# Six PSUM banks as three score tiles and three transposed groups where attention scores are narrow

## The chip, the cores and the metric

The kernel runs on one core of one Trainium2 chip. A core has five engines that run their own instruction streams and wait for each other through semaphores: TensorE (PE in the profile; PEld is its weight load), VectorE (DVE), ScalarE (ACT), GpSimd (POOL) and SyncE (SP), which issues the DMAs here. Matrix products land in PSUM, eight banks of 512 float32 columns for each of 128 partitions; everything else lies in SBUF or in device memory. The metric is the device time of one execution in microseconds (us), as the median of several runs.

## The reference, cut to what matters

One layer: a gated feed-forward block, a token mixer with two attentions side by side, and a second feed-forward block, for 1024 tokens and 1024 channels in float32. The two attentions are what the change touches.

```python
# differential attention: 8 heads, two score maps each, causal
s = einsum('bqhcd,bkhcd->bhcqk', qb, k) * scale          # c = 0, 1
p = softmax(where(kpos <= qpos, s, NEG_INF))
a = p[:, :, 0] - lam * p[:, :, 1]
o = einsum('bhqk,bkhe->bqhe', a, v)
...
# sparse attention: 16 heads in 2 groups, three branches with gates
o_cmp = ...   # over compressed blocks of keys
o_slc = ...   # causal, over selected key blocks (with 16 blocks in all, every causal one)
o_win = ...   # causal, over a window of 512 keys
o = g[..., 0:1] * o_cmp + g[..., 1:2] * o_slc + g[..., 2:3] * o_win
```

For query block i of 128 rows a causal score map has w = 128 * (i + 1) columns, from 128 to 1024; the window's has at most 640.

## The kernel before, in words

Float32 products are made of two parts of each operand, a rounded one ("hi") and the rest ("lo"), so most matrix products appear three times (L52, L53, L54). The phases follow each other: the first feed-forward block, preliminaries of the mixer (projections, the compressed branch), the differential attention `da_phase`, the sparse attention `ns_phase`, the output projections, the second feed-forward block.

Both attention phases have the same shape. The work of a head is cut into four steps m of two query blocks (z = 0, 1). `scores` makes one score map of one query block: matmuls into a PSUM tile S (L871), on VectorE the mask and the row minimum (L878, in place in S), on ScalarE the exponential (L880), which reads S and writes the probabilities to SBUF (Pt in the differential phase; Ps and Pw, selected and window branch, in the sparse one). That read is the last use of S. `tr_split` then transposes up to four 128x128 blocks of probabilities into one PSUM bank (tr, L926) and splits them into th (ScalarE, L89) and tl (VectorE, L85); matmuls with the values add them up in another bank, o (L948 to L950 in the differential phase, L1083 and L1084 in the sparse one; L1049 starts the sparse o with the compressed branch). The scores of step m are written into the program ahead of `finish` of step m - 1, the part with the transposes, so scores run ahead of the products.

Between the steps a `Filler` puts projections that later phases need: 24 matmuls into one bank (gm), a few of them after each query block. They have a lower priority than the attention's instructions, and each is held behind the last score matmul emitted so far (`K.gate = K.last`). In the differential phase they are many, in the sparse phase few: six matmuls a query block.

A Tile framework makes semaphores and order: it takes the program's instructions by priority (mostly their order in the program) as soon as their operands and a buffer of their pool are ready in its own model of time, and the order that it so finds for each engine is fixed in the compiled program. A pool has a number of buffers; a tile waits until one is free. Pools are opened with `reuse_waits="tile"`: where a new pool takes the space of a closed one, its tiles wait for the tiles that lay there.

PSUM during both attentions, before: two score tiles of two banks each (`sp1`, `sp2`), two transposed groups (`tr1`, `tr2`), one o, one gm, on the left side one after the other. A score map of more than 512 columns fills half of each of two banks; a narrower one lies in the first bank only. During the preliminaries four banks on the right side belong to `gm0`, and the other four on the left; the last projections of the preliminaries are emitted at the head of `da_phase`, still in `gm0`, before `cg.close()` closes that pool. Each of them is emptied by VectorE through single SBUF buffers that are stored to device memory.

SBUF buffers around it: 7 score rows (Pt) in the differential phase and 5 of each kind in the sparse one; 2 and 3 buffers each of th and tl.

Of the kernel before, what the change touches and what calls it, by code (L numbers as in the profile page):

```python
# [7 lines left out]
F32 = mybir.dt.float32  # L8
# [10 lines left out]
P = 128  # L19
T = 1024  # L20
TB = 512
# [22 lines left out]
def open_pool(K, ctx, name, bufs, psum=False, side=None):  # L44
    kw = {"space": PSUM} if psum else {}
    if side:
        kw["side"] = side
    return ctx.enter_context(K.tc.tile_pool(name=name, bufs=bufs, reuse_waits="tile", **kw))
# [813 lines left out]
        nc.sync.dma_start(out=K.s_pc[u * 2 + pr][tb], in_=pp.bitcast(F32))  # L862


def scores(K, passes, w, mask, nm, pt, l):
    nc = K.nc
    S = K.sp.tile([P, T], F32, tag="S", name="S")
    pieces = [(0, 0, w)] if w <= TB else [(0, 0, w // 2), (TB, w // 2, w // 2)]
    for o, c, n in pieces:
        for i, (q, k, k0) in enumerate(passes):  # L870
            K.last = nc.tensor.matmul(S[:, o:o + n], lhsT=q, rhs=k[:, k0 + c:k0 + c + n], start=i == 0, stop=i == 1)  # L871
    if w <= TB:
        sv, mv, pv = S[:, 0:w], mask, pt[:, 0:w]
    else:
        sv = S.rearrange("p (b c) -> p b c", b=2)[:, :, 0:w // 2]
        mv = mask.rearrange("p (b c) -> p b c", b=2)
        pv = pt[:, 0:w].rearrange("p (b c) -> p b c", b=2)
    nc.vector.tensor_tensor_reduce(out=sv, in0=sv, in1=mv, scale=-0.125, scalar=BIG, op0=ALU.add, op1=ALU.min,  # L878
                                   accum_out=nm)
    return nc.scalar.activation(out=pv, in_=sv, func=AF.Exp, scale=-1.0, bias=nm, accum_out=l)  # L880
# [81 lines left out]
def da_finish2(K, h, H, ob, sq):  # L962
    nc = K.nc
    tot = K.tr.tile([P, TB], F32, tag="tr", name="tot")
    nc.tensor.matmul(tot, lhsT=K.ones, rhs=sq, start=True, stop=True)
    m = K.op.tile([P, TB], F32, tag="sq", name="m")
    nc.vector.tensor_scalar(out=m, in0=tot, scalar1=1.0 / P, scalar2=EPS, op0=ALU.mult, op1=ALU.add)
    y = K.op.tile([P, TB], F32, tag="yr", name="yr")
    z = K.op.tile([P, TB], F32, tag="zr", name="zr")
    newton_rsqrt(nc, y, z, m, nc.gpsimd)  # L970
    nc.vector.scalar_tensor_tensor(out=ob, in0=ob, scalar=K.hgain[:, h:h + 1], in1=y, op0=ALU.mult, op1=ALU.mult)
    yo = [K.op.tile([P, TB], F32R, tag=t, name="yo") for t in ("yr", "zr")]
    split(nc, yo[0], yo[1], ob)
    for i in range(2):
        nc.sync.dma_start(out=K.s_yda[H][h][:, i], in_=yo[i].bitcast(F32))


def da_load(K, h):
    drain([da_load_parts(K, h)])
# [320 lines left out]
TR_DA = 2  # L1300
# [4 lines left out]
def da_phase(K, cg):  # L1305
    nc = K.nc
    with ExitStack() as ctx:
        K.kp, K.vp, K.qp = open_pool(K, ctx, "dk", B_DK), open_pool(K, ctx, "dv", B_DV), open_pool(K, ctx, "dq", B_DQ)
        K.nk, K.vv = {}, {}
        for n, f in enumerate(da_units(K, 0)[:2] + da_units(K, 1)):  # L1310
            if n == 2:
                early = da_load_parts(K, 0)
            if n >= 2:
                next(early)
            if n == 5:
                q0 = da_queries(K, 0, 0)
            drain([f()])
        cg.close()
        K.low = LOW_DA
        log_exp(K)  # L1320
        K.pp, K.sm, K.tp, K.op = (open_pool(K, ctx, "dp", B_DP), open_pool(K, ctx, "dsm", 6), open_pool(K, ctx, "dt", B_DT),
                                  open_pool(K, ctx, "do", 1))
        K.sp = open_pool(K, ctx, "sp1", 2, True)
        K.tr = open_pool(K, ctx, "tr1", TR_DA, True)
        K.ops = open_pool(K, ctx, "o1", 1, True)
        K.gm = open_pool(K, ctx, "gm1", 3 - TR_DA, True)
        pend = K.fin = None

        def finish(h, m, res):
            if m % 2 == 0:  # L1330
                K.o = K.ops.tile([P, TB], F32, tag="o", name="o")
            if K.fin:
                da_finish2(K, *K.fin)
                K.fin = None
            da_pv(K, h, m, res, K.o)
            if m % 2 == 1:
                K.fin = da_finish(K, h, m // 2, K.o)

        ng = NG_DA // 2
        W = K.A["win"]  # L1340
        units = []
        for p in (2, 3):
            cs = [[C_QDA + 2 * p, C_QDA + 2 * p + 1], [C_KDA + 2 * p, C_KDA + 2 * p + 1], [C_VDA + 2 * p], [C_VDA + 2 * p + 1]]
            units += [(f, [W[c] for c in ws]) for f, ws in zip(da_units(K, p), cs)]
        units += [(f, [W[C_GATE + c]]) for c, f in enumerate(gate_units(K, range(16)))]
        units += [(lambda d=d: pda_unit(K, d), [K.A["wda"][d]]) for d in range(KD)]
        fill = K.filler = Filler(K, units)
        for p in range(4):
            fill.pace(4 * (p + 1) if p < 2 else 8 + ng * (p - 1), PACE_DA)
            for h in (2 * p, 2 * p + 1):  # L1350
                if h:
                    da_load(K, h)
                for m in range(4):
                    qt = q0 if h + m == 0 else da_queries(K, h, m)
                    if h == 4:
                        ns_load_key(K, m)
                    res = da_scores(K, h, m, qt, fill.step)
                    if pend:
                        finish(*pend)
                    pend = (h, m, res)  # L1360
            fill.end()
        finish(*pend)
        da_finish2(K, *K.fin)


def ns_phase(K):
    nc = K.nc
    K.low = LOW_NS
    with ExitStack() as ctx:
        K.wslab = open_pool(K, ctx, "wsl", 1).tile([P, 5 * P], F32, name="wslab")  # L1370
        nc.sync.dma_start(out=K.wslab, in_=K.A["wslab"])
        K.qp, K.kp, K.pcp = open_pool(K, ctx, "nq", 2), open_pool(K, ctx, "nk", 1), open_pool(K, ctx, "npc", B_NPC)
        K.pp, K.sm, K.tp, K.op = (open_pool(K, ctx, "np", B_NP), open_pool(K, ctx, "nsm", 6), open_pool(K, ctx, "nt", B_NT),
                                  open_pool(K, ctx, "no", B_NO))
        K.sp = open_pool(K, ctx, "sp2", 2, True)
        K.tr = open_pool(K, ctx, "tr2", 2, True)
        K.ops = open_pool(K, ctx, "o2", 1, True)
        K.gm = open_pool(K, ctx, "gm2", 1, True)
        fill = K.filler
        fill.pace(8 + 16 + KD, PACE_NS)  # L1380
        ns_load_values(K)
        pend = None

        def finish(hd, m, res, st, g, par):
            if m % 2 == 0:
                K.o = K.ops.tile([P, TB], F32, tag="o", name="o")
            ns_pv(K, hd, m, res, K.o, st[0], g, par)
            if m % 2 == 1:
                ns_fold(K, par, K.o, st[1])
                if par:  # L1390
                    ns_out(K, hd // 2, m // 2, st[1])

        for g in range(2):
            for pr in range(4 * g, 4 * g + 4):
                for H in range(2):
                    pc = K.pcp.tile([P, 2, TB], F32R, tag="pc", name="pc")
                    nc.sync.dma_start(out=pc.bitcast(F32), in_=K.s_pc[pr][H])
                    y = K.op.tile([P, TB], F32, tag="y", name="y")
                    for par in range(2):
                        hd = pr * 2 + par  # L1400
                        qt = []
                        for z in range(2):
                            t = K.qp.tile([P, TB], F32R, tag=f"q{z}", name="qt")
                            nc.sync.dma_start(out=t.bitcast(F32), in_=K.s_qns[hd // 4][z:z + 2, :, hd % 4, :, H * TB:(H + 1) * TB]
                                              .rearrange("h a d t -> (h a) d t"))
                            qt.append(t)
                        for m in (2 * H, 2 * H + 1):
                            res = ns_scores(K, hd, m, qt, g, fill.step)
                            if pend:
                                finish(*pend)  # L1410
                            pend = (hd, m, res, (pc, y), g, par)
        fill.end()
        if pend:
            finish(*pend)


def proj(K, open_x, after):
# [54 lines left out]
def body(tc, A, out):  # L1472
    nc = tc.nc
    K = Ctx()
    K.tc, K.nc, K.A = tc, nc, A
    K.low, K.vv, K.gate, K.fill, K.seen = 0, {}, None, None, {}
    K.h, K.acc, K.R = [None] * 2, [None] * 2, [None] * 2
    with ExitStack() as ctx:
        const = open_pool(K, ctx, "const", 1)
# [172 lines left out]
```

## Time and profile before

| | |
|---|---|
| median of 3 runs | 2951.38 us (2950.32 to 2952.54) |
| the profiled execution | 2957.75 us, span 2955.7 us |
| TensorE busy | 2830.8 us, 96% of the span |
| VectorE, ScalarE, GpSimd busy | 68%, 46%, 27% |
| mean granted TensorE clock | 0.986 |
| first and last score matmul (L871) of the differential phase | 972.0 us, 1449.1 us |
| last score matmul of the sparse phase | 2070.4 us |

A row of the timeline holds the start in us, the duration in us, engine, line and operation, the tiles (out<-in), the shape, how many instructions are merged ("x4"), and in brackets the idle time of the engine before it and what ended it. A row of the table of stretches holds start and end, then the busy us of each engine with the number of instructions, the granted clock, the share of the DMA engines and GB/s. A row of the waits holds engine, line and what it waited for, the us in total, how many times, and the longest.

### The profile page before, as it was taken

Reading aid. Unit: us, or ns where it says so; the run is one execution under the profiler, and the core shown is the slowest. Engines: PE = TensorE matmul, PEld = TensorE weight load, DVE = VectorE, ACT = ScalarE, POOL = GpSimd, SP = SyncE. Lnnn points to the kernel's source line nnn. Section 1 sums busy time; section 2 is a strip of 40 time slices with the busy share of each in tenths; the row PEclk is TensorE's granted clock in tenths of the full one; section 3 lists DMA queues with packets and bytes.
Section 4 is the critical chain, followed back from the end, with each engine's and each line's share of the span. In section 5 each row is a group of like instructions: output and inputs, shape, how many; then the busy total and the mean of one; then the engine's idle time right before and its main releaser. Section 6 shows DMA issues by size and latency. Waiting matters only on the chain. (4 is left out here: it accounts for less than half of the span.)

```text
span 2955.7 us, 40158 instructions
## 1 busy us (share of the span) xinstructions
PE 2830.8 (96%) x14276; PEld 2129.2 (72%) x14276; DVE 2002.1 (68%) x3347; ACT 1366.1 (46%) x2347; POOL 788.7 (27%) x701
## 2 busy tenths in 40 slices
PE   8999999999999899989899999999999999999998
PEld 6644447888888678778788888888778854444886
DVE  7866856666687467667677777776343877675666
ACT  7543424442332245445466666666332653342443
POOL 3133321000144123322233323332242413333001
PEclk9999999999999999999999999999999999999999
DMA  4355548655456544444332234222742246454854
GB/s 161 129 194 180 182 161 287 214 172 170 146 200 240 173 161 168 170 165 164 122 115 79 86 119 155 79 84 76 281 158 100 89 147 230 149 185 158 297 182 146
DMA packets 212711, 478.20 MB, mean 162 GB/s; under 512 B 20896, under 2 KB 39584, under 8 KB 212512
## 3 DMA queue, kind: packets, MB, share of 16 engines
q1 hardware_dynamic: 212512, 475.65, 47.1%
q8 instruction: 112, 1.84, 0.3%
q14 instruction: 87, 0.71, 0.1%
HBM read 313.56 MB, written 162.00 MB: 161 GB/s over the span
## 5 line engine op out<-in xcount | busy, mean ns | idle before, releaser
L405 PEld LDWEIGHTS <-w 128*128 128x128 f16 x3024 | 297.1, 99 | 381.1 <-issue 30.4
L52 PE MATMUL gm<-hi,whi 128*128 128x512 f32 x880 | 351.5, 399 | 4.0 <-ACT whi L89 1.6
L54 PE MATMUL gm<-hi,wlo 128*128 128x512 f32 x880 | 348.3, 397 | 1.1 <-DVE wlo L85 1.1
L53 PE MATMUL gm<-lo,whi 128*128 128x512 f32 x880 | 348.0, 395 | 0.0
L405 PE MATMUL Y<-tf,w 128*128 128x512 f16 x1296 | 296.7, 383 | 19.1 <-DVE u L443 15.6
L871 PE MATMUL S<-kt,qt 128*128 128x320 f32 (+5 forms) x1152 | 274.6, 352 | 37.5 <-ACT Pt L880 12.0
L85 DVE TENSOR_TENSOR tl<-tr,th 128x512 fp32r<-128x512 f32 (+2 forms) x384 | 236.3, 619 | 89.0 <-ACT th L89 85.5
L89 ACT ACTIVATE th<-tr 128x512 fp32r<-128x512 f32 (+2 forms) x384 | 203.7, 542 | 200.4 <-PE tr L926 195.6
L85 DVE TENSOR_TENSOR wlo<-st,whi 128x1024 fp32r<-128x1024 f32 x154 | 197.6, 1300 | 113.5 <-ACT whi L89 112.2
L878 DVE CUSTOM_DVE_ANT_0 S<-S,slab 128x896 f32<-128x896 f32 (+7 forms) x320 | 224.7, 709 | 65.8 <-PE S L871 61.3
L53 PE MATMUL acc<-wlo,whi 128*128 128x512 f32 (+1 forms) x628 | 244.1, 389 | 1.0 <-DVE wlo L85 1.0
L89 ACT ACTIVATE whi<-st 128x1024 fp32r<-128x1024 f32 x154 | 160.7, 1057 | 178.2 <-PE acc L54 111.6
L54 PE MATMUL acc<-whi,wlo 128*128 128x512 f32 (+1 forms) x628 | 242.8, 389 | 0.0
L52 PE MATMUL acc<-whi 128*128 128x512 f32 (+1 forms) x628 | 240.4, 387 | 0.0
L871 PEld LDWEIGHTS S<-kt,qt 128*128 128x128 f32 x1152 | 183.4, 190 | 61.5 <-ACT Pt L880 13.8
L1037 POOL TENSOR_SCALAR Ps<-Ps,l 128x384 f32<-128x384 f32 (+7 forms) x128 | 100.7, 787 | 428.6 <-DVE l L1035 214.4
L405 PE MATMUL X<-h,w 128*128 128x512 f16 x864 | 195.3, 379 | 0.5 <-ACT s L415 0.5
L52 PEld LDWEIGHTS gm<-hi,whi 128*128 128x128 f32 x880 | 168.3, 191 | 37.2 <-ACT whi L89 2.2
L54 PEld LDWEIGHTS gm<-hi,wlo 128*128 128x128 f32 x880 | 167.8, 191 | 37.3 <-DVE wlo L85 1.8
L53 PEld LDWEIGHTS gm<-lo,whi 128*128 128x128 f32 x880 | 168.1, 191 | 30.9
L85 DVE TENSOR_TENSOR wlo<-wst,whi 128x1024 fp32r<-128x1024 f32 x103 | 135.8, 1320 | 45.4 <-ACT whi L89 36.1
L1083 PE MATMUL o<-th,vt 128*128 128x256 f32 (+1 forms) x608 | 165.0, 288 | 1.6 <-ACT th L89 1.5
(320 smaller groups left out, 6128.7 us busy)
## 6 DMA issues: line engine op xcount, KB each, us to landing
wst<-in_win_dram SPq DMA_DIRECT2D x55, 512.0 KB
sw<-w2s SPq DMA_DIRECT2D x44, 512.0 KB
st<-sw SPq DMA_DIRECT2D x88, 256.0 KB
st<-saT SPq DMA_DIRECT2D x88, 256.0 KB
a<-in_f1w_dram SPq DMA_DIRECT2D x36, 512.0 KB
a<-in_f2w_dram SPq DMA_DIRECT2D x36, 512.0 KB
st<-saB SPq DMA_DIRECT2D x66, 256.0 KB
qt<-sq SPq DMA_DIRECT2D x128, 128.0 KB
```

The costliest lines, as they stand in the source:

```text
L52: first = nc.tensor.matmul(out, lhsT=w[0][:, wk], rhs=x[0], start=start, stop=False, skip_group_check=skip)
L53: nc.tensor.matmul(out, lhsT=w[0][:, wk], rhs=x[1], start=False, stop=False, skip_group_check=skip)
L54: nc.tensor.matmul(out, lhsT=w[1][:, wk], rhs=x[0], start=False, stop=stop, skip_group_check=skip)
L85: return nc.vector.tensor_tensor(out=lo, in0=src, in1=hi.bitcast(F32), op=ALU.subtract)
L89: nc.scalar.activation(out=hi, in_=src, func=AF.Copy)
L405: K.mark = nc.tensor.matmul(o, lhsT=w[:, a, m * h + k], rhs=x[k][:, b], start=start and k == 0 and i == 0, stop=k == h - 1 and i == 2, ski ...
L871: K.last = nc.tensor.matmul(S[:, o:o + n], lhsT=q, rhs=k[:, k0 + c:k0 + c + n], start=i == 0, stop=i == 1)
L878: nc.vector.tensor_tensor_reduce(out=sv, in0=sv, in1=mv, scale=-0.125, scalar=BIG, op0=ALU.add, op1=ALU.min, accum_out=nm)
L1037: nc.gpsimd.tensor_scalar(out=p[:, 0:n], in0=p[:, 0:n], scalar1=l[:, c:c + 1], scalar2=1.0, op0=ALU.mult, op1=ALU.mult)
L1083: nc.tensor.matmul(dst, lhsT=v, rhs=hi[:, b * P:(b + n) * P], start=False, stop=False, skip_group_check=True)
```

## The change

`scores` takes its tile from a new function `score_tile`. It keeps two layouts of six banks: for w up to 512 three score tiles of one bank and three transposed groups, for wider ones two score tiles of two banks and two groups as before. Where the layout of the wanted tile isn't the open one, both pools are closed and opened anew, on the right side of PSUM. o and gm stay open, on the left side, which puts them in banks 0 and 1. In the differential phase steps m = 0, 1 of a head are narrow and m = 2, 3 wide; in the sparse phase the first half of the queries (two heads, m = 0, 1) is narrow and the second half wide, as the window's 640 columns are wide too. So the layout changes twice in each of 8 heads of the one and twice in each of 8 pairs of heads of the other. The transposes of a step are emitted after the next step's scores, so they take their group from the layout of that next step.

```diff
+def score_tile(K, w):
+    n = 1 if w <= TB else 2
+    if K.s_banks != n:
+        close_scores(K)
+        K.sp, K.s_banks = open_pool(K, K.s_ctx, "sp", (3, 2)[n - 1], True, side="right"), n
+        K.tr = open_pool(K, K.s_ctx, "tr", (3, 2)[n - 1], True, side="right")
+    return K.sp.tile([P, n * TB], F32, tag="S", name="S")
+
+
+def close_scores(K):
+    K.s_ctx.close()
+    K.s_ctx, K.s_banks = ExitStack(), 0
+
+
 def scores(K, passes, w, mask, nm, pt, l):
     nc = K.nc
-    S = K.sp.tile([P, T], F32, tag="S", name="S")
+    S = score_tile(K, w)
...
 # da_phase
-        K.sp = open_pool(K, ctx, "sp1", 2, True)
-        K.tr = open_pool(K, ctx, "tr1", TR_DA, True)
...
         da_finish2(K, *K.fin)
+        close_scores(K)
...
 # ns_phase
-        K.sp = open_pool(K, ctx, "sp2", 2, True)
-        K.tr = open_pool(K, ctx, "tr2", 2, True)
...
             finish(*pend)
+        close_scores(K)
...
 # body
+    K.s_ctx, K.s_banks = ExitStack(), 0
```

## The prediction

> **What bounds the kernel now.** I read the page first, then the table of stretches cut at each change of score width, then the waits of TensorE, then the timeline at three places.
>
> ```profile
> span 2955.7 us, 40158 instructions
> PE 2830.8 (96%) x14276; PEld 2129.2 (72%) x14276; DVE 2002.1 (68%) x3347; ACT 1366.1 (46%) x2347; POOL 788.7 (27%) x701
> ```
>
> TensorE (PE) is the bound: no other engine passes 68%. The change alters no matmul, so all it can move is PE's idle time while the two attentions run, from about 968 to 2109 us. The vector engine's score operation (L878) shows the widths, and I cut there. The four sums are: differential attention narrow (up to 512 columns) and wide, sparse attention narrow and wide, eight stretches each; under them one neighbouring pair of the sparse phase.
>
> ```profile
> core 0: us, PE busy (x) PEld busy (x) DVE busy (x) ACT busy (x) POOL busy (x), PEclk, DMA share, GB/s
> sum 254.20, PE 230.55 PEld 196.51 DVE 159.83 ACT 104.47 POOL 63.36; mean PE 28.82 PEld 24.56 DVE 19.98 ACT 13.06 POOL 7.92
> sum 249.90, PE 232.77 PEld 194.11 DVE 178.50 ACT 128.66 POOL 66.70; mean PE 29.10 PEld 24.26 DVE 22.31 ACT 16.08 POOL 8.34
> sum 295.50, PE 276.40 PEld 240.99 DVE 200.12 ACT 169.94 POOL 77.25; mean PE 34.55 PEld 30.12 DVE 25.01 ACT 21.24 POOL 9.66
> sum 336.30, PE 330.56 PEld 298.59 DVE 250.32 ACT 221.68 POOL 110.61; mean PE 41.32 PEld 37.32 DVE 31.29 ACT 27.71 POOL 13.83
> 1539.50:1578.20 38.70, 35.99 (x233) 31.48 (x233) 26.87 (x77) 21.61 (x57) 9.90 (x16) 1.00 0.21 78
> 1578.20:1616.10 37.90, 37.47 (x246) 34.13 (x244) 30.69 (x70) 26.08 (x54) 13.80 (x16) 1.00 0.27 90
> ```
>
> Sum less PE busy is PE's idle time: 23.7 and 17.1 us in the differential phase, 19.1 and 5.7 us in the sparse one. The pair shows the pattern there: a narrow stretch idles 2.7 us, a wide one 0.4 us. So 42.8 us of idle lie where buffers are added. Next, what ended PE's waits, first from 1477.7 to 2037.9 us (sparse), then from 974 to 1477 us (differential).
>
> ```profile
> PE S L871 <- ACT Ps L880: 7.1, 14, 1.0
> PE o L1049 <- DVE y L1093: 5.2, 7, 1.1
> PE o L1084 <- DVE tl L85: 4.0, 15, 0.3
> PE S L871 <- ACT Pw L880: 3.3, 8, 0.9
> PE o L1083 <- ACT th L89: 0.7, 4, 0.2
> ```
>
> ```profile
> PE S L871 <- ACT Pt L880: 12.0, 8, 5.7
> PE o L948 <- ACT th L89: 6.8, 2, 3.9
> PE tr L653 <- DVE vt L650: 3.7, 2, 2.6
> ```
>
> A score matmul that waits for an exponential (Ps, Pw, Pt, L880) waits for a score tile to come free: 10.4 us in the sparse phase. In the differential phase it is 12.0 us, but one wait of 5.7 us is half of that, and it stands behind ScalarE, which waits there for the store of a filler's tile:
>
> ```profile
> 1269.37 0.60 ACT L89 ACTIVATE vh<-tr 128x512 fp32r<-128x512 f32 x1 [5.61 <-DMA sv<-vh]
> ```
>
> **The change part by part.** It adds and removes no engine instruction and no DMA; it changes which tile waits for which.
>
> *Three score tiles where they are narrow.* The clearest case is the step from wide to narrow:
>
> ```profile
> 1538.96 0.44 PE L871 MATMUL S<-kt,qt 128*128 128x128 f32 x2 [0.22 <-ACT Ps L880]
> 1540.51 0.44 PE L871 MATMUL S<-kt,qt 128*128 128x128 f32 x2 [0.78 <-ACT Ps L880]
> 1539.99 0.37 ACT L880 ACTIVATE Ps<-S,nm 128x128 f32<-128x128 f32 x1 [0.22 <-DVE nm L878]
> 1543.87 0.79 ACT L880 ACTIVATE Pw<-S,nm 128x640 f32<-128x640 f32 x1
> ```
>
> The last wide tile is held until ScalarE reads it at 1543.87, so the second narrow tile waits for the first one's exponential (1539.99), 0.78 us. In the new layout one freed wide tile makes room for two narrow ones, and this wait goes. The 10.4 us are the most that goes; nothing is the least, if the next wait ends as late: the third tile again waits for 1543.87. I take 6.5 us, nearer to the upper end, because the 0.78 us recur in each sparse narrow stretch and the wide stretches, where PE has other work, idle so little. The Trainium skill ("Perfetto Trace Analysis", Optimization Strategy) says that the same gap repeating on the engine that should be saturated can mean that there isn't enough SBUF or PSUM for the next tile. By it the whole idle of the eight sparse stretches, 19.1 us, would fall to the wide ones' 0.4 us each, a gain of 15.9 us in place of my 8 us (this edit and the next), and the sum below would be -16 us.
>
> *Three transposed groups.* The waits for th and tl in the sparse phase are 4.0 + 0.7 us. A third PSUM group helps only until the split's output, which keeps its three buffers there (two in the differential phase); the 5.2 us of L1049 wait for the output bank, which stays single. Bounds: 4.7 us gained, or 2 us lost (half of the tl waits again) when PE's order puts transposes ahead of products. I take a gain of 1.5 us.
>
> *Other narrow waits of the differential phase.* Here the fillers' 24-matmul products keep PE fed. Bounds: the 5.7 us wait goes and so does a second of its kind (3.9 us), or one more such wait arises (4 us lost). I take a gain of 2 us, the 12.0 us less 5.7 us, a third of it.
>
> *The new wait at a switch.* Six banks as 3 + 3 and as 4 + 2 overlap in one bank: a transposed group of the narrow layout sits where half of a wide score pair will be. Whether a new pool waits for the old pool as a whole or tile by tile shows at the old boundary between the phases: the sparse phase's mask, the first tile in the space of the closed pools, is loaded while their last scores still run.
>
> ```profile
> L1371 SPq DMA_DIRECT2D wslab<-in_wslab_dram x1: 424/424/424, 1442.6 to 1442.6; - x1
> 1449.09 1.17 PE L871 MATMUL S<-kt,qt 128*128 128x512 f32 x4
> ```
>
> So I take it tile by tile. Then one wide pair is free at once and the other waits for the last narrow group. What that means in the sparse phase:
>
> ```profile
> 1577.40 0.74 PE L871 MATMUL S<-kt,qt 128*128 128x320 f32 x4
> 1579.48 0.86 PE L871 MATMUL S<-kt,qt 128*128 128x320 f32 x4
> 1579.70 0.80 ACT L880 ACTIVATE Ps<-S,nm 128x640 f32<-128x640 f32 x1
> 1581.97 0.51 PE L926 MATMUL tr<-ident,Pw 128*128 128x128 f32 x3
> 1584.38 0.55 DVE L85 TENSOR_TENSOR tl<-tr,th 128x384 fp32r<-128x384 f32 x1
> ```
>
> The last narrow group of the sparse phase here is the one transposed at 1581.97. Until its tl is split the second wide score (1579.48) has only the first pair, whose exponential ends at 1580.50: 1.0 us later than now. Behind it on PE stand the filler matmuls that are gated by it, the later scores, and through them the vector engine's L878. Products of older heads stand ready, which cover part: bounds 0 and 1.0 us for each of the eight switches, and I take 0.6 us, 5 us in all. In the differential phase:
>
> ```profile
> 1089.82 1.29 PE L871 MATMUL S<-kt,qt 128*128 128x512 f32 x6
> 1105.44 0.49 PE L926 MATMUL tr<-ident,Pt 128*128 128x128 f32 x3
> ```
>
> The last narrow group (1105.44) comes 15 us after the first wide score, so scores are held to one pair for that long; but they are issued there one or two at a time between filler products of 5.3 us (24 matmuls at 0.222 us, a row below), and one pair passes a tile in less (3.1 us from the matmul at 1577.40 to the end of its exponential at 1580.50). I take 1 us for all eight, bounds 0 and 8 us (the sparse phase's price).
>
> *The start.* Before, the first scores use banks 0 to 3, free since the preliminaries, while the last preliminary products (gm0) use 4 to 7. After the change the scores lie on the right side, in gm0's banks, and wait until gm0's last tile. That moves 6.3 us of score matmuls behind these products, and takes away what the early scores cost:
>
> ```profile
> 972.05 0.45 PE L871 MATMUL S<-kt,qt 128*128 128x128 f32 x1 [4.31 <-issue]
> 977.83 0.66 PE L871 MATMUL S<-kt,qt 128*128 128x128 f32 x2 [4.26 <-DMA kt<-sk]
> 977.80:985.00 7.20, 7.17 (x25) 5.92 (x26) 2.02 (x6) 0.46 (x2) 0.37 (x1) 0.75 0.76 253
> 985.00:1001.00 16.00, 16.00 (x72) 13.23 (x72) 4.25 (x6) 2.70 (x3) 2.54 (x2) 1.00 0.50 174
> 993.42 1.23 DVE L85 TENSOR_TENSOR rl<-m,rh 128x1024 fp32r<-128x1024 f32 x1 [12.25 <-DMA sq<-rl]
> 994.75 0.69 DVE L625 TENSOR_TENSOR m<-gm,cR 128x512 f32<-128x512 f32 x1
> ```
>
> The 6.3 us are five rows of score matmuls from 974 to 1036.3 us, of which the first and the last stand here with busy us behind the bar:
>
> ```profile
> L871 PE MATMUL S<-kt,qt 128*128 128x384 f32 x12 | 2.4, 335 | 0.0
> L871 PE MATMUL S<-kt,qt 128*128 128x128 f32 x2 | 0.7, 430 | 4.3 <-DMA kt<-sk 4.3
> ```
>
> PE stands 4.31 + 4.26 us behind scores whose keys have not landed, and runs at a granted clock of 0.75 for 7.2 us after it (1.8 us): 10.4 us. What is late next: without the scores PE fills gm0's four banks, 4 x 24 matmuls at 0.222 us (72 in 16.00 us), from 967.7 to 989, but the vector engine empties the first only with two operations from 994.75 to 996, because it waits for a store (993.42). So about 7 us idle and 1.7 us of low clock come back. The gain is some 2 us, and half of the 3.7 us that L653 waits for a vector engine busy with scores: I take 4 us. Bounds: the whole 10.4 us gained; or 6 us lost, since the moved 6.3 us of scores no longer fill PE's waits here.
>
> The sum: -6.5 - 1.5 - 2 + 5 + 1 - 4 = -8 us. The profiled execution took 2957.75 us (span 2955.7), 6.4 us more than the median of 2951.38 us; the same gain from the median gives **2943 us**. All lower and all upper ends together would be -35 and +28 us.
>
> **The rivals.**
> *No change (within 0.2%, 5.9 us, about what a measurement of this kernel can tell from none).* The third tile only moves PE's wait on to the next thing that is late: the exponential of 1543.87 stands behind a transposed group's split on ScalarE, and more score tiles do not make that earlier. The two rows of 1539 and 1540 speak for it, the 0.4 us of idle in wide stretches with two tiles against it. With 3 us instead of 6.5 us from the scores the sum is -4.5 us, 2947 us. The Trainium skill ("TensorE: Matmul & The Clock Gate", HAM oscillation) tells of a kernel to which "Adding PSUM double-buffering gave no further gain"; by it the time would stay at 2951 us. What the trace has against it is 19.1 us of idle in 295.5 us, 6.5%, in the sparse narrow stretches.
>
> *Slower: the switch drains the scores.* If a pool's first tile waits for all tiles of the old pools, each step from narrow to wide waits for the last narrow group's split. In the sparse phase that moves the first wide score from 1577.40 to 1584.9, about 7.5 us, of which PE can fill some 5 us with the older products; 2.5 us of idle x 8 is 20 us in place of 5. The differential phase has fillers and pays perhaps 1 us x 8, 7 us above my value. Sum: -8 + 15 + 7 = +14 us, 2965 us. It decides from 0.9 us a switch: 16 of them are then 14 us, which is all that the other terms gain. Against it speaks the mask's early load.
>
> *A larger gain.* The early scores' stall goes without a new one (10.4 us in place of 4) and the score waits go whole (10.4 in place of 6.5): -18 us, 2933 us. For it: the stores that hold the start may issue earlier when the queue is less full.
>
> **How the numbers follow.** The forecast has 0.40 (2938 to 2947 us by itself, some of it within 0.2%), the larger gain 0.16, no change 0.18, the drain or a worse order of instructions 0.26. The compiled order of all engines is made anew with other buffers, and the waits of 3.9 and 5.7 us in the differential phase can fall otherwise, a few us either way; so the range runs from 2925 us (the larger gain and one such wait less) to 2963 us (just short of the drain's full price), leaving 1 in 10 on each side. Faster by over 0.2% (below 2945.5 us): the larger gain and most of the forecast, 0.50. Within: 0.24. Slower: 0.26.
>
> **What would show it.** Right: no score waits of 0.8 us at the second narrow tile; idle of a sparse narrow stretch near 1.5 us instead of 2.7; wide ones 0.4 to 1 us; no score before the last gm0 product, and no wait for kt there. Wrong: waits of S for DVE tl at the start of wide stretches, wide stretches idle over 2 us (the drain); narrow stretches as idle as before with waits for th, tl or y in place of Ps (no change); PE idle over 8 us between 968 and 1040 (the start).

## The result, and the profile after

The changed kernel takes 2980.61 us (median of 4 runs, 2976.54 to 2984.01) against 2951.96 us before (2950.32 to 2955.25, 4 runs): ratio 1.0095, 95% interval 1.0078 to 1.0113. That is 28 us slower, where 8 us faster were forecast, and outside the range. The profiled execution has a span of 2977.8 us. Where differences are given in us below, they are the ratio less one, times 2952 us.

Lines below `score_tile` stand 14 further down than before (scores L885, transposes L940, products L962 and L1097), in kernels with a few lines more 15 or 16.

First the page of the kernel after, then its table of stretches, cut as before at each change of score width (order of the sums: differential narrow, differential wide, sparse narrow, sparse wide), and one neighbouring pair of the sparse phase:

```profile
span 2977.8 us, 40127 instructions
PE 2825.1 (95%) x14276; PEld 2127.8 (71%) x14276; DVE 1998.3 (67%) x3347; ACT 1366.9 (46%) x2347; POOL 789.4 (27%) x701
```

```profile
sum 264.80, PE 210.88 PEld 174.82 DVE 136.67 ACT 97.66 POOL 47.77; mean PE 26.36 PEld 21.85 DVE 17.08 ACT 12.21 POOL 5.97
sum 222.60, PE 211.89 PEld 178.28 DVE 177.10 ACT 127.02 POOL 78.36; mean PE 26.49 PEld 22.29 DVE 22.14 ACT 15.88 POOL 9.79
sum 281.50, PE 266.02 PEld 239.09 DVE 204.16 ACT 172.68 POOL 86.99; mean PE 33.25 PEld 29.89 DVE 25.52 ACT 21.59 POOL 10.87
sum 334.20, PE 328.45 PEld 296.53 DVE 246.75 ACT 217.56 POOL 101.65; mean PE 41.06 PEld 37.07 DVE 30.84 ACT 27.19 POOL 12.71
1628.50:1666.40 37.90, 37.45 (x248) 34.14 (x247) 30.05 (x71) 25.80 (x53) 12.06 (x15) 1.00 0.25 89
1666.40:1701.20 34.80, 34.55 (x233) 31.27 (x233) 26.74 (x77) 21.95 (x58) 10.14 (x18) 1.00 0.27 86
```

The two phases went opposite ways. The sparse phase fell from 631.8 us (295.5 + 336.3) to 615.7 us, and its narrow stretch here idles 0.25 us where a neighbouring one idled 2.7 us. The differential phase ends 43 us later: the first sparse score operation moved from 1477.7 to 1521.1 us. TensorE (PE) idles 53.9 us in the differential narrow stretches, against 23.7. These two sums don't cover quite the same work, since the first narrow stretch begins at 1033.7 us here and at 973.6 before; over the whole of it, from 960 us to the first sparse score operation, PE idles 79.9 us against 45.1. The waits name what for, first in the differential phase (974 to 1520 us), then in the sparse one (1521.1 to 2068.1 us):

```profile
PE o L962 <- DMA vt<-sv: 25.1, 5, 11.1
PE gm L52 <- DVE vl L85: 14.5, 3, 11.0
PE gm L52 <- ACT whi L89: 10.9, 1, 10.9
```

```profile
PE o L1098 <- DVE tl L85: 13.6, 18, 7.0
PE S L885 <- ACT Pw L894: 2.2, 8, 0.4
PE S L885 <- ACT Ps L894: 1.0, 1, 1.0
PE S L885 <- DVE tl L85: 0.8, 1, 0.8
```

In the sparse phase the waits of score matmuls for exponentials fell from 10.4 to 3.2 us, and the new wait at a switch (S for tl) is 0.8 us in all; of the 13.6 us for tl half is one wait of 7.0 us in the first stretch. In the differential phase none of the three large waits is one that the prediction had, and those that it had are gone: S for Pt fell from 12.0 to 0.3 us, o for th from 6.8 to 1.5. The longest in detail: timeline of the kernel after, PE alone, then the DMA queue (SP) at the same place.

```profile
1362.31 0.27 PE L964 MATMUL o<-th,vt 128*128 128x128 f32 x1
1363.93 1.12 PE L979 MATMUL tot<-sq,ones 128*128 128x512 f32 x2 [1.35 <-ACT sq L972]
1364.89 0.49 PE L940 MATMUL tr<-ident,Pt 128*128 128x128 f32 x3
1376.53 0.55 PE L962 MATMUL o<-th,vt 128*128 128x256 f32 x1 [11.14 <-DMA vt<-sv]
1376.88 0.41 PE L963 MATMUL o<-tl,vt 128*128 128x256 f32 x1
1377.09 1.27 PE L885 MATMUL S<-kt,qt 128*128 128x320 f32 x4
```

```profile
1361.37 4.55 SPq L904 DMA_DIRECT2D qt<-sq  x4
1366.01 1.64 SPq L724 DMA_DIRECT2D smx<-vt  x1
1367.73 1.16 SPq L1009 DMA_DIRECT2D vt<-sv  x2
```

V of a head has one pair of buffers (`B_DV = 2`, hi and lo), so the next head's V can be loaded only when the last product of the head before (1362.31) has read it. SP issues the load at 1367.73, behind query loads and a store, and the data are there at 1376.5. PE has only the total and three transposes to do meanwhile; the wide scores (128x320) stand behind the product that waits. The same place in the kernel before, PE and then SP:

```profile
1343.61 0.28 PE L950 MATMUL o<-th,vt 128*128 128x128 f32 x1
1343.72 1.39 PE L871 MATMUL S<-kt,qt 128*128 128x320 f32 x8
1344.95 0.39 PE L52 MATMUL gm<-hi,whi 128*128 128x512 f32 x1
...
1347.70 1.02 PE L965 MATMUL tot<-sq,ones 128*128 128x512 f32 x2
1348.55 0.49 PE L926 MATMUL tr<-ident,Pt 128*128 128x128 f32 x3
1348.80 1.66 PE L871 MATMUL S<-kt,qt 128*128 128x384 f32 x8
1350.30 0.39 PE L52 MATMUL gm<-hi,whi 128*128 128x512 f32 x1
...
1353.28 0.36 PE L948 MATMUL o<-th,vt 128*128 128x256 f32 x1
```

```profile
1343.80 0.92 SPq L995 DMA_DIRECT2D vt<-sv  x2
```

Here four wide score maps (16 matmuls) and two pieces of filler lie between the last product of one head and the first of the next, and the 9.5 us from 1343.80 to 1353.28 cover the load without a wait. So the change moved scores and fillers in PE's order. The programs show how much. For the 15 switches of the differential phase I counted the older groups, that is the tiles of the `tr` pool (transposed groups and totals) that stand ahead of the first score of the new layout in the program but behind it on PE:

```
                              narrow to wide      wide to narrow
before                        1 2 2 2 2 2 2 3     4 4 2 2 2 2 4
the change                    0 0 0 0 0 0 0 0     0 0 0 0 0 0 0
```

Before, the first score overtook some of them at every switch, to wide and back to narrow; after, at none.

### The profile page after: what moved, and what is told of

Its sections match the earlier page's. It is cut to its first block, busy times and chain, and to the rows that moved or that the text cites. A ratio compares the mean times of both kernels' runs of the same rounds, so it can differ in the third digit from the quotient of the medians.

```text
span 2977.8 us, 40127 instructions
## 1 busy us (share of the span) xinstructions
PE 2825.1 (95%) x14276; PEld 2127.8 (71%) x14276; DVE 1998.3 (67%) x3347; ACT 1366.9 (46%) x2347; POOL 789.4 (27%) x701
## 5 line engine op out<-in xcount | busy, mean ns | idle before, releaser
L52 PE MATMUL gm<-hi,whi 128*128 128x512 f32 x880 | 354.4, 403 | 30.3 <-DVE vl L85 14.5
L885 PE MATMUL S<-kt,qt 128*128 128x320 f32 (+5 forms) x1152 | 262.2, 349 | 12.9 <-DMA qt<-sq 4.2
L52 PEld LDWEIGHTS gm<-hi,whi 128*128 128x128 f32 x880 | 168.7, 192 | 64.9 <-ACT whi L89 13.4
L885 PEld LDWEIGHTS S<-kt,qt 128*128 128x128 f32 x1152 | 185.4, 192 | 29.7 <-ACT Pt L894 4.6
L1098 PE MATMUL o<-tl,vt 128*128 128x256 f32 (+1 forms) x608 | 159.2, 294 | 15.5 <-DVE tl L85 15.3
```

The source lines that it names most:

```text
L52: first = nc.tensor.matmul(out, lhsT=w[0][:, wk], rhs=x[0], start=start, stop=False, skip_group_check=skip)
L1098: nc.tensor.matmul(dst, lhsT=v, rhs=lo[:, b * P:(b + n) * P], start=False, stop=last, skip_group_check=True)
```

## The experiments

Theory A was that the bank shared by both layouts, which lies under the first wide score tile, holds that score. Theory B: the late start drags the rest. Theory C: the sparse phase gains only from work done ahead. The kernels ran in four groups (e1 to e4; e5, e6, e8, e9; e10 to e13; e14 and e15), each on one chip with runs of the kernel before beside it.

| kernel | median us | ratio to before | 95% interval | us |
|---|---|---|---|---|
| e1_ns_only | 2933.47 | 0.9933 | 0.9920 to 0.9945 | -20 |
| e2_da_only | 3005.10 | 1.0175 | 1.0161 to 1.0189 | +52 |
| e3_tr_first | 2995.31 | 1.0142 | 1.0128 to 1.0156 | +42 |
| e4_right_side | 2970.66 | 1.0066 | 1.0052 to 1.0080 | +19 |
| e5_start_free | 2965.22 | 1.0041 | 1.0028 to 1.0053 | +12 |
| e6_da_scores3 | 2952.56 | 0.9996 | 0.9987 to 1.0005 | -1 |
| e8_scores4 | 2985.90 | 1.0112 | 1.0098 to 1.0126 | +33 |
| e9_no_v | 2945.85 | 0.9970 | 0.9960 to 0.9979 | -9 |
| e10_before_no_v | 2947.24 | 0.9993 | 0.9984 to 1.0003 | -2 |
| e11_drain_alone | 2982.85 | 1.0106 | 1.0091 to 1.0122 | +31 |
| e12_ns_2s3t | 2924.90 | 0.9915 | 0.9901 to 0.9929 | -25 |
| e13_ns_3s2t | 2967.44 | 1.0061 | 1.0048 to 1.0073 | +18 |
| e14_ns_2s4t | 2924.57 | 0.9898 | 0.9883 to 0.9913 | -30 |
| e15_split | 2952.20 | 0.9992 | 0.9982 to 1.0002 | -2 |

**The phases apart.** e1_ns_only opens the old pools in `da_phase`, e2_da_only in `ns_phase`; `score_tile` leaves them alone there:

```diff
+    if K.s_banks == 9:
+        return K.sp.tile([P, T], F32, tag="S", name="S")
# da_phase (e1) or ns_phase (e2)
+        K.s_banks = 9
+        K.sp = open_pool(K, ctx, "sp1", 2, True)
+        K.tr = open_pool(K, ctx, "tr1", TR_DA, True)
```

> The new layout in the sparse phase alone; the differential phase keeps its two score tiles of two banks, two transposed groups and their places. Theory A (the loss of the change lies in the differential phase alone, where a wide score waits for a bank of a narrow transposed group; the sparse phase gains 16 us, 631.8 us to 615.7 us): 2952 - 16 = 2936 us, and the differential phase stays within 3 us of its 505 us. Theory B (the loss comes from the start, where the first scores wait for the preliminary products): the start is as before, so 2936 us as well. Theory C (the sparse phase only gained because the differential phase had left it work done ahead): 2952 us.

> The new layout in the differential phase alone. Theory A and theory B: 2952 + 43 = 2995 us, with gaps of TensorE of about 11 us before a product that waits for the load of V (vt<-sv). Theory C: 2981 us, as with the whole change.

The sparse phase alone gains 20 us, the differential phase alone loses 52 us; together 32 us, close to the 28 us of the change. C is out.

**The shared bank.** e3_tr_first opens `tr` ahead of `sp`, so that the first wide score tile lies over banks of narrow score tiles alone.

> The whole change, but at each switch the pool of transposed groups is opened ahead of the score pool. The bank that both layouts share is then in the second wide score tile instead of the first, so the first wide score has only banks of narrow score tiles under it. The start changes a little too: the first score tile lies in a bank that the preliminary products don't use, the second one in one that they do. Theory A: the first wide score and the products gated by it go ahead of the older step's products again, the waits of about 11 us for V go, 2940 us (the 16 us of the sparse phase less some us of the second tile's wait). Theory B or three narrow tiles as such: the waits for V stay, 2975 to 2985 us.

Theory A as I put it fell: the order on PE is that of the change (0 older groups at each of the 15 switches), and the two waits for V are 12.1 and 10.5 us. Of the 42 us, 12 are a wait for another load behind the attentions, which the traces of before and of the change don't have:

```profile
PE pj L52 <- DMA yl<-syn: 12.2, 1, 12.2
```

**The start.** e4_right_side moves only the pools of the kernel before; e5_start_free is the whole change with the differential phase's pools on the left:

```diff
# e4: da_phase of the kernel before
-        K.sp = open_pool(K, ctx, "sp1", 2, True)
-        K.tr = open_pool(K, ctx, "tr1", TR_DA, True)
+        K.sp = open_pool(K, ctx, "sp1", 2, True, side="right")
+        K.tr = open_pool(K, ctx, "tr1", TR_DA, True, side="right")
# e5: da_phase of the change; score_tile opens on the left there
-        K.ops = open_pool(K, ctx, "o1", 1, True)
-        K.gm = open_pool(K, ctx, "gm1", 3 - TR_DA, True)
+        K.ops = open_pool(K, ctx, "o1", 1, True, side="right")
+        K.gm = open_pool(K, ctx, "gm1", 3 - TR_DA, True, side="right")
```

> The kernel before, in which only the two pools of the differential phase are put on the right side of PSUM, so that its first scores wait for the preliminary products as in the change; no pool is switched, two score tiles of two banks and two transposed groups throughout. Theory A: only the start moves, which by the gaps and the half clock of both traces between 960 and 1040 us costs about 3 us: 2955 us (2950 to 2960). Theory B: most of the 43 us of the differential phase appear here, 2985 us or more.

> The whole change with its switched pools of the differential phase on the left side of PSUM (banks 0 to 5) and o and gm on the right (6 and 7): the first scores have free banks again, everything else is as in the change. Theory D (a new layout's first score can stand in TensorE's order only behind the last transposed group of the old layout, since its pool is opened when the old one has been closed; in the compiled order of the change no wide score stands ahead of an older narrow group, in the kernel before two to four groups stand behind it at each switch; this costs about 34 us in the differential phase, and the late start the 17 us of e4_right_side): 2953 + 34 - 20 = 2967 us. Theory B (the late start drags the rest): 2935 to 2945 us. Theory E (the place of the pools matters to neither, the 17 us came from elsewhere): 2980 us.

The late start costs 19 us by e4 and 16 us by e5 (28 less 12); e5 came out where the sum of start and order put it, and theories B and E fall. The first 80 us of the phase, in the kernel before and then in e4:

```profile
960.00:1040.00 80.00, 66.30 (x287) 53.81 (x286) 37.59 (x71) 21.82 (x39) 12.88 (x13) 0.91 0.49 168
```

```profile
960.00:1040.00 80.00, 62.68 (x259) 49.57 (x258) 27.71 (x37) 14.80 (x19) 10.51 (x8) 0.89 0.45 153
```

PE is busy for 3.6 us less and at a lower clock (0.02 of 80 us, 1.6 us at most), so some 5 us of the start's price are seen there. The rest comes later in the same phase. The first sparse score operation of e4 stands at 1495.4 us instead of 1477.7, and from 960 us to it PE idles 60.5 us against 45.1, in smaller waits that hardly stood there before (gm for vt 6.1 us against 0.3, the total for sq 6.2 against 0.8). Why a late start brings these stays open. In e5 that operation comes at 1516.5 us, only 4.6 us ahead of the change's 1521.1, while the two spans differ by 14.4 us: the sum of start and order fits the times, but not stage by stage.

**The order alone.** Theory D: a score pool that covers a bank of the old groups lets none of its scores go ahead of these groups. e11_drain_alone has that with two score tiles and two groups throughout; the narrow ones lie in banks 0 to 3, the wide scores over all four:

```diff
-        K.sp, K.s_banks = open_pool(K, K.s_ctx, "sp", (3, 2)[n - 1], True, side="right"), n
-        K.tr = open_pool(K, K.s_ctx, "tr", (3, 2)[n - 1], True, side="right")
+        K.sp, K.s_banks = open_pool(K, K.s_ctx, "sp", 2, True), n
+        K.tr = open_pool(K, K.s_ctx, "tr", 2, True)
```

> The differential phase with as many buffers as before (two score tiles, two transposed groups, wide or narrow) but with both pools closed and opened at each switch, so that the narrow groups lie in banks 2 and 3, which the wide score pool (banks 0 to 3) covers; start and sparse phase as in the kernel before. In its compiled order, as in that of the change, no first wide score stands ahead of an older narrow group. Theory D (that order alone costs the differential phase some 34 us, with waits of about 11 us for vt<-sv): 2954 + 34 = 2988 us. Rival (the additional buffers cause the loss): 2954 us, no wait for V over 3 us.

31 us, as D had it, without one buffer more than before. D explains the switches to wide alone. At those back to narrow the new scores cover no bank of an old group, in the change as in e11, and yet no older group stands behind them (in e11 two do at the first of the seven); why is open. The waits of e11 from 974 to 1520 us:

```profile
PE o L964 <- DMA vt<-sv: 30.7, 4, 10.6
```

**Is it V's load?** e9_no_v and e10_before_no_v leave out the loads of V for heads 1 to 7, in the change and in the kernel before:

```diff
+    if h:
+        K.vv[h] = K.vv[0]
+        return
     K.v = []
```

> The change without the loads of V for heads 1 to 7 of the differential phase: all heads use head 0's V (this part of the computation is left out), so no product waits for vt<-sv. Theory D with V as the wait that the drain lays bare: the two waits of 11 us, two of 1.3 us and the half clock of 13.7 us behind each of the two long ones go, 24.5 + 13.7 = 38 us less than the change, 2942 us. Rival (V is only the first of several late tiles, th, sq or ob are as late): 10 us less or nothing, 2970 us or more.

> The kernel before without the loads of V for heads 1 to 7 of the differential phase (all heads use head 0's V; this part is left out), as the counterpart of e9_no_v. If V's load is hidden in the kernel before (one wait of 2.95 us in its trace): 2948 to 2954 us, so that the 35 us that e9_no_v took from the change are the price of the order. If the loads cost by their traffic: 2925 us or less, and most of the 35 us says nothing of the change.

Without the loads the change falls by 37 us (1.0095 to 0.9970) and the kernel before by 2, which the interval can't tell from none. So the load was hidden before, and uncovering it is what the order costs. My 38 us were put together wrongly: half clock during a wait costs nothing, so the waits give 24.5 us and some 5 us of slow work behind them. The wait of 11 us of gm for vl went too (14.5 to 3.2 us), and the scores' wait for queries grew (4.2 to 11.8 us); together that is 33 of the 37 us.

**Which buffer does it.** e6_da_scores3 switches in the differential phase only the score pool (three to two tiles, two fixed groups; the sparse phase as in the change). e8_scores4 switches in both phases only the score pool, four to two. e12 to e14 are e1 with other numbers for the narrow layout:

```diff
-(3, 2)[n - 1] ... (3, 2)[n - 1]      # score tiles ... groups
+(2, 2)[n - 1] ... (3, 2)[n - 1]      # e12
+(3, 2)[n - 1] ... (2, 2)[n - 1]      # e13
+(2, 2)[n - 1] ... (4, 2)[n - 1]      # e14
```

> In the differential phase only the score pool is switched, between three tiles of one bank and two of two banks, on the left side (banks 0 to 3); two transposed groups, o and gm stay open on the right. The sparse phase is as in the change. The old score tiles are all ahead of the new ones in the program, so nothing is drained: in the compiled order two to four older groups stand behind the first score of each new layout, as in the kernel before. Theory D: no waits of 11 us for V, the differential phase as before or some us better, 2925 to 2934 us. Rival (three narrow score tiles by themselves let the products run ahead of V's load): waits for V stay, 2950 us or more.

> In both phases only the score pool is switched, between four tiles of one bank and two of two banks; two transposed groups throughout, in the differential phase placed so that the start is as before. Theory F (the sparse phase's gain of 20 us comes from the score tiles): 2925 to 2935 us. Theory G (it needs the third transposed group): the sparse phase falls back by 8 us or more against e1_ns_only, 2940 us or more.

> As e1_ns_only (the sparse phase alone), but narrow steps have two score tiles and three transposed groups. Theory G (the third group gives the gain): 2934 us as with three and three. Theory F (the third score tile gives it): 2945 to 2954 us.

> As e1_ns_only, but narrow steps have three score tiles and two transposed groups. Theory F: 2934 us. Theory G: 2945 to 2954 us, as e8_scores4 had no gain in the sparse phase with four score tiles and two groups. If each of the two edits gives half, both kernels come out near 2944 us.

> As e12_ns_2s3t (the sparse phase alone), with four transposed groups where scores are narrow, which uses all six banks. If the number of groups still limits the narrow steps: 2915 to 2920 us. If the next wait is the split's three output buffers (th, tl), as the prediction had it: 2925 us, the same as with three groups.

The third score tile loses wherever it comes without a third group: 18 us in the sparse phase (e13), some 19 us in the differential one (e6 against e1), where the order on PE is free (1 to 4 older groups behind the first score at each of the 15 switches); with four tiles in both phases it is 33 us (e8). The third group gains 25 us by itself (e12), more than both edits (20 us, though the intervals overlap). A fourth group, 30 us, can't be told from a third (overlapping intervals). The waits of the sparse phase, over the same stretches as before, e12 first and e13 second:

```profile
PE o L1100 <- DVE tl L85: 4.0, 13, 0.3
PE o L1065 <- DVE y L1109: 2.3, 3, 0.9
PE S L887 <- ACT Pw L896: 2.3, 8, 0.5
...
PE S L887 <- ACT Ps L896: 0.2, 1, 0.2
```

```profile
PE o L1100 <- DVE tl L85: 13.3, 40, 1.7
PE o L1065 <- DVE y L1109: 8.4, 8, 1.1
PE o L1099 <- ACT th L89: 4.2, 16, 0.4
PE S L887 <- ACT Ps L896: 2.3, 7, 0.3
```

With two score tiles and three groups the score waits for exponentials fall from 10.4 to 2.5 us; with three score tiles and two groups they fall to 3.5 us (1.2 us for Pw not shown), but the products wait 25.9 us for th, tl and y, against 9.9 before. Over the whole sparse phase PE idles 33.6 us in e13 against 24.8, which is about half of the 18 us. In e6 the products' waits for th rise in the same way, from 6.8 to 17.0 us in the differential phase:

```profile
PE o L963 <- ACT th L89: 17.0, 6, 7.8
PE S L886 <- ACT Pt L895: 13.5, 11, 3.1
```

The score waits there (S for Pt) follow the groups too. They are 12.0 us before, 13.5 with the third tile alone (e6) and 12.9 with the held order alone (e11), but 0.3 in the change and 1.0 in e15 below, which has two score tiles and three groups.

**A pool or a tile.** e15_split has two score tiles as two pools of one tile each, three groups where narrow, in both phases, started as in e5. Only the second wide tile covers a bank of the old groups:

```diff
+        K.s_banks, K.s_at = n, 1
+        K.sp = [open_pool(K, K.s_ctx, f"sp{z}", 1, True, side=K.s_side) for z in range(2)]
...
+    K.s_at += 1
+    return K.sp[K.s_at % 2].tile([P, n * TB], F32, tag="S", name="S")
```

> Both phases with two score tiles, and three transposed groups where they are narrow; the two score tiles are two pools of one tile each, so that only the second wide one covers a bank of the narrow groups; the differential phase is placed so that the start is as before. In the compiled order of the differential phase the first wide score has one or two older groups behind it again at about half of the switches. If the pool that covers an old group's bank is what drains, and the drain of the second score alone is cheap: the differential phase is as before and the sparse phase gains 25 us, 2925 to 2930 us. If the second score's drain, behind which the gated products stand, costs as much as the first's: 2950 - 25 + 31 = 2956 us.

Its waits for V from 974 to 1520 us:

```profile
PE o L964 <- DMA vt<-sv: 21.8, 3, 9.8
```

The first wide score overtakes again at five of the eight switches to wide (1 0 0 2 0 2 2 2 older groups behind it). So closing both pools at once isn't by itself what holds it; this fits a hold that belongs to the pool over the bank, not to the tile, and with that e3 as well. But the time barely gains: 2952 us, 23 us above e12, and three waits for V remain. The second score of a query block, it seems, drains as the first one did, and the fillers are gated by it (`K.gate = K.last`); that wasn't measured by itself.

e12 and e14 beat both kernels: 2924.9 and 2924.6 us, 0.9915 and 0.9898 of the kernel before.

## Why the prediction was wrong

*Three narrow score tiles, -6.5 us.* The sign failed: +18 us by itself in the sparse phase (e13), and beside a third group still +5 us or nothing (e1 against e12, overlapping intervals). The step read a wait named by the exponential as the want of a score tile. The scores were late because of what stood ahead of them: with a third group and still two score tiles that wait all but goes (e12). Scores that may run further ahead, with groups that can't follow, push the products back (25.9 us of product waits in e13 against 9.9).

*Three transposed groups, -1.5 us.* The direction was right, the size wrong by more than ten: -25 us (e12). The bound of 4.7 us came from the waits for th and tl alone. It missed the score waits, and it missed that idle time isn't all. The whole sparse phase before, and then in e12:

```profile
1477.70:2109.50 631.80, 606.96 (x3869) 539.58 (x3869) 450.44 (x1154) 391.62 (x901) 187.86 (x259) 0.99 0.32 109
```

```profile
1477.80:2084.90 607.10, 594.14 (x3872) 532.99 (x3872) 445.09 (x1154) 392.35 (x900) 191.13 (x259) 1.00 0.33 113
```

PE's idle time falls by 11.9 us (24.8 to 13.0), and its busy time by 12.8 us, for the same matmuls. Matmuls overlap in these records (PE's rows at 1343.61 and 1343.72 begin 0.11 us apart, and the first shows 0.28 us); busy time is their union, so it also shrinks when matmuls stand closer. Some 3 of the 12.8 us are the clock: before, PE worked 6.3 us at half clock from 1769.9 to 1776.7 us, and in e12 no stretch of the phase is at half clock. The Trainium skill ("Perfetto Trace Analysis", the note at its head) calls matmul busy time a bad metric because matmuls are pipelined; this pair of rows agrees, and my limit of 42.8 us of idle was no limit. The Trainium skill's rule on repeating gaps ("Perfetto Trace Analysis", Optimization Strategy), by which the sparse phase would gain 15.9 us, came nearer (16.1 us between the traces of before and of the change) than my 8 us. That is partly luck: by the rule all of it would be idle time, and idle time fell by 3.6 us (24.8 to 21.2), the rest being busy time.

*Other narrow waits of the differential phase, -2 us.* These waits went, and further than forecast: S for Pt from 12.0 to 0.3 us, o for th from 6.8 to 1.5. But the third score tile isn't what took them away: with it alone they are 13.5 and 17.0 us (e6), and with a third group and two score tiles 1.0 and 5.4 (e15). The time that this is worth can't be read in the change, where the held order costs more.

*The new wait at a switch, +5 us sparse and +1 us differential.* This step failed most. In the sparse phase it costs 0.8 us of waits. In the differential phase the order that comes with it costs 31 us (e11). I priced a score that starts later in an unchanged order, and named gated fillers only for the sparse phase. What counts is what those scores and fillers covered: V's load, 9 us long. It was in the trace of before, as the wait of 3.0 us that did show in one head out of seven. The rival of a drain had the mechanism, but put 20 of its 28 us into the sparse phase, and its test, a load into SBUF issued while old tiles were still in use, was true and beside the point: waits by tile don't say what the compiled order allows a pool.

*The start, -4 us.* Wrong in sign: +16 to +19 us. That no score stands ahead of the last preliminary product came true, and the two waits of 4.3 us at the first scores went. The sign of failure that I named, idle over 8 us between 968 and 1040 us, told nothing: it is 15.2 us in the change, but it was 13.4 before. The kernel after:

```profile
991.84 1.06 ACT L89 ACTIVATE rh<-m 128x1024 fp32r<-128x1024 f32 x1 [22.68 <-DMA sq<-rh]
993.07 1.23 DVE L85 TENSOR_TENSOR rl<-m,rh 128x1024 fp32r<-128x1024 f32 x1 [21.54 <-DMA sq<-rl]
999.90 1.99 ACT L89 ACTIVATE whi<-wst 128x1024 fp32r<-128x1024 f32 x2
1000.99 0.80 PE L52 MATMUL gm<-hi,whi 128*128 128x512 f32 x1 [10.95 <-ACT whi L89]
```

I saw the store that holds the vector engine, and took 7 us of idle until it empties a bank. The last release is ScalarE's split of the next weights, which stands behind its own store (22.68 us of waiting) and rh: 10.95 us. The bound of 6 us lost looked at these 80 us alone, and 11 to 14 us come later.

*What to look for.* Right: no score wait of 0.8 us at a second narrow tile (one of 1.0 us stands at a later tile at the head of the sparse phase, 1522.1); sparse narrow stretches at about 0.8 us of idle (seven of them, 5.4 us), better than the 1.5 named. Wrong: the sum, since -16 us in the sparse phase met +43 in the differential one.

## What to carry to other kernels

Ask of every buffer change what the compiled order will be, not only which tile waits: here a score pool opened over a bank of the old groups held all its scores behind them, and the price was that of the load which the held work had covered. A wait that names the reader of a buffer isn't yet a want of that buffer; in the sparse phase a buffer more for the consumer's side (transposed groups) gained 25 us where one more for the producer's side (score tiles) lost 18 us. Where one phase of a kernel gains and another loses, give each its own layout.

## What was not expected of the hardware

Each of the four waits of about 11 us in the change came with exactly the same stretch of half clock. The table of stretches shows them (granted clock after the busy times):

```profile
992.30:1006.00 13.70, 4.78 (x11) 3.32 (x12) 9.68 (x12) 3.54 (x4) 4.15 (x4) 0.50 0.70 248
1296.10:1309.80 13.70, 5.35 (x13) 4.20 (x14) 2.81 (x5) 3.21 (x6) 0.69 (x1) 0.50 0.58 197
1367.70:1381.40 13.70, 4.87 (x17) 4.39 (x18) 3.10 (x7) 2.65 (x6) 3.65 (x3) 0.50 0.54 167
1425.80:1439.50 13.70, 4.78 (x17) 4.30 (x18) 2.73 (x5) 3.14 (x6) 1.88 (x2) 0.50 0.53 166
```

13.70 us at 0.50, of which PE worked 4.8 to 5.4 us: by my estimate half of that, some 2.5 us, is lost after each wait, on top of it. The Trainium skill ("TensorE: Matmul & The Clock Gate", Part 1) has the clock come back after about 3.4 us of sustained work; here it took 4.8 us and more. The trace shows why the two need not differ. In its clock record these four stretches last 13.65 us, and all the shorter ones 3.41, 6.83 or 10.24 us (only the one at the end of the program is cut short): whole multiples of 3.41 us. Each wait ended 1.3 to 1.8 us before the last 3.41 us of its stretch began, so full clock came after one such piece that was all but full of work.
